# Raw block products ahead of the token sums in a seven-product down projection, and attention buffers in another order

## The chip, the cores and the metric

The kernel runs on one core of one Trainium2 chip. The metric is the device time of one execution in microseconds (us); lower is better. Before the change it is 1193.19 us, the median of three runs (1192.18 to 1194.01).

## What is computed

One layer of a hybrid encoder on 256 tokens of width 2048, everything in float32:

```python
def reference(x, ...):
    h = rms_norm(x, attn_norm[layer])
    x = x + hybrid_mixer(h, ...)        # w_in, two groups of 8 heads, w_out
    h = rms_norm(x, ffn_norm[layer])
    x = x + conv_ffn(h, ...)

def conv_ffn(h, w_up_l, conv_w_l, conv_b_l, w_down_l):
    u = h @ w_up_l                      # 2048 -> 2 * 5632
    u = causal depthwise conv, width 3 (u) + conv_b_l
    gate, val = jnp.split(u, 2, axis=-1)
    return (jax.nn.silu(gate) * val) @ w_down_l     # 5632 -> 2048
```

The mixer is a projection `w_in` (2048 to 6152 columns), softmax attention with forget gates for eight heads, stick-breaking attention for eight more, and a projection `w_out` of the normed, joined outputs.

## The kernel before

**Precision.** Each weight block arrives from memory as float32 (`w_raw`, 128 x 2048 elements, 1 MB) and is split by `split` (lines 204 to 213) into a high part `w_hi`, a cast on ScalarE (line 208), and a low part `w_lo = w_raw - w_hi`, a subtraction on VectorE (line 209). Activations are split in the same way. A product is then three matmuls: high by high, high by low, low by high. `load` (198 to 202) issues the DMA on SyncE's queue (SP). Loads and splits are traced inside `tc.high_priority(offset=AHEAD)` with `AHEAD = 200`, so that the framework's scheduler ranks them as if they stood 200 instructions earlier. The scheduler fixes the order on every engine when the kernel is built; on the chip each engine follows its list in order and waits on semaphores.

**Buffers.** `tc.tile_pool` takes a stretch of SBUF for tiles of equal tags that rotate through `bufs` buffers. A pool opened after others have closed lies over their memory, and its tiles wait until what was there is done. In the attention stage (`ExitStack` at 272) there are, in order, `wpool` (three `w_raw`, two `w_hi`, two `w_lo`), `at` (queries, keys, values, and the outputs `oT` and sums `ssq`) and `tmp` (temporaries, among them the tag "raw" that `sums_of_squares` writes with its `junk`). After it closes, `wff` (574) is opened in the same place, with four `w_raw`, three `w_hi`, three `w_lo` and one `w_sum`.

**Stages.** `w_in` and the attention heads; `w_out` in two groups (545 to 566), the second of which also makes the sums of squares and the transposed rows `hT` for the next norm; then the feed-forward part. The latter goes through 44 blocks of 128 features in six parts (`FFN_PARTS`): five of eight blocks, one of four. For each two blocks `up_pair` computes gate and value by `feature_major` (244 to 262, matmuls at 252 and 257), in two halves of 1024 input features; `convolved` does the convolution on ScalarE and VectorE; lines 765 to 769 make SiLU, the product `gate`, and its split `g2`, appended to `pairs`. From the third pair on, `combinations` (637 to 654) makes sums and differences of two pairs' token halves in `t` and splits them into `s` (lines 650 and 651); its calls make `sums[0]` (first and third pair) and `sums[1]` (second and fourth).

**The down projection runs behind.** When a part is done, its down projection is put into `behind`, and `step` (616 to 626), called after each half of `feature_major`, advances it: 14 products in the 16 halves of the next part (`pace` 14), 11 pieces in the 8 halves of the last (`pace` 22). `down_in_seven` (656 to 734) treats the part's four pairs as 2 x 2 blocks and replaces eight block products by seven of 12 matmuls each (`product`, line 675). In order, by the names used below:

- M1: weights `w11`, tokens `of_pairs(0, 0)`; M2: `w11 + w12` with `of_sums(0)`; M3: `w22` with `of_sums(2)`
- M4: `w11 + w12 + w22` with `of_sums(1)`; M5: `w12 + w22` with `of_sums(3)`
- M6: `w21` with `of_pairs(1, 0)`; M7: `w11 + w12 + w22 + w21` with `of_pairs(1, 1)`

The running sum of weights is the tile `w_sum` (one buffer), loaded with `w11` and added to on VectorE at 698, 706 and 726. `of_sums` reads `sums[0]` in the first six of its twelve matmuls and `sums[1]` in the last six; `of_pairs(1, 0)` likewise reads the third pair's `g2` and then the fourth's. `down_in_seven` runs nine times in all, each covering 1024 of the 2048 output columns; the fifth part's other 1024 columns and the last part are plain products.

Of the kernel before, what the change touches and what calls it, by code (L numbers as in the profile page):

```python
# [8 lines left out]
F32 = mybir.dt.float32  # L9
F32R = mybir.dt.float32r  # L10
AF = mybir.ActivationFunctionType
ALU = mybir.AluOpType
AX = mybir.AxisListType

P = 128
D = 2048
S = 256
# [3 lines left out]
NH = 8  # L21
# [22 lines left out]
def hybrid_layer(  # L44
# [20 lines left out]
    act, dve = nc.scalar, nc.vector  # L65
# [10 lines left out]
    psb = ctx.enter_context(tc.tile_pool(name="psb", bufs=2, space=bass.MemoryType.PSUM))  # L76

    def f32(t):
        return t.bitcast(F32)
# [37 lines left out]
    def rsqrt(out_, ss, scale, n):  # L117
        a = small.tile([P, n], F32, name="rs_a", tag=f"rs_a{n}")
        y = small.tile([P, n], F32, name="rs_y", tag=f"rs_y{n}")
        u = small.tile([P, n], F32, name="rs_u", tag=f"rs_u{n}")  # L120
        dve.tensor_scalar(a, ss, scale, EPS, op0=ALU.mult, op1=ALU.add)
        act.activation(y, a, AF.Ln)
        act.activation(y, y, AF.Exp, scale=-0.5)
        dve.tensor_tensor(u, a, y, op=ALU.mult)
        dve.tensor_tensor(u, u, y, op=ALU.mult)
        dve.tensor_scalar(u, u, -0.5, 1.5, op0=ALU.mult, op1=ALU.add)
        dve.tensor_tensor(out_, y, u, op=ALU.mult)
# [31 lines left out]
    def sums_of_squares(ss, c):  # L159

        for t in range(NT):
            junk = tmp.tile([P, 512], F32, name="junk", tag="raw", bufs=4)
            act.activation(junk, xt[t][:, c * 512 : (c + 1) * 512], AF.Square, accum_out=ss[:, t, c : c + 1])

    def token_factors(ss, n):
# [30 lines left out]


    def load(src, into=None):
        raw = into if into is not None else wpool.tile([P, 2048], F32, name="w_raw", tag="w_raw")
        a, b = src.shape[1:]  # L200
        nc.sync.dma_start(raw[:, : a * b].rearrange("p (a b) -> p a b", a=a), src)
        return raw

    def split(raw, a, b):
        hi = wpool.tile([P, 2048], F32R, name="w_hi", tag="w_hi", bufs=n_split)
        lo = wpool.tile([P, 2048], F32R, name="w_lo", tag="w_lo", bufs=n_split)
        n = a * b
        act.copy(hi[:, :n], raw[:, :n])  # L208
        dve.tensor_tensor(lo[:, :n], raw[:, :n], f32(hi[:, :n]), op=ALU.subtract)  # L209
        return (  # L210
            hi[:, :n].rearrange("p (a b) -> p a b", a=a),
            lo[:, :n].rearrange("p (a b) -> p a b", a=a),
        )
# [5 lines left out]
    def rows_of(w, k0, n, c0, cols):  # L219
        return w[k0 * P : (k0 + n) * P, c0 : c0 + cols].rearrange("(k p) c -> p k c", p=P)  # L220
# [49 lines left out]
        return t2  # L270

    with ExitStack() as actx:
        n_split = 2
        wpool = actx.enter_context(tc.tile_pool(name="wpool", bufs=3))
        at = actx.enter_context(tc.tile_pool(name="at", bufs=1))
        pss = actx.enter_context(tc.tile_pool(name="pss", bufs=2, space=bass.MemoryType.PSUM))
        tmp = actx.enter_context(tc.tile_pool(name="tmp", bufs=2))

        def project(c0, cols, **kw):
            return token_major(lambda k: hT[:, k], wi, 0, KT, c0, cols, **kw)  # L280

        def scaled(dst, ps, t):
            act.activation(dst, ps, AF.Identity, scale=rstd1[:, t : t + 1])
# [8 lines left out]
        def fox_rows(acc, dst, g):  # L292

            rows = []
            for t in range(NT):
                raw = tmp.tile([P, 512], F32, name="raw", tag="raw", bufs=4)
                scaled(raw, acc[:, t, :], t)
                rows.append(raw)
            for t in range(NT):
                raw = rows[t]  # L300
                r3 = raw.rearrange("p (h d) -> p h d", h=4)
                sq = tmp.tile([P, 512], F32, name="sq", tag="raw", bufs=4)
                dve.tensor_tensor(sq, raw, raw, op=ALU.mult)
                ss = small.tile([P, 4], F32, name="ss", tag="ss")
                dve.tensor_reduce(ss, sq.rearrange("p (h d) -> p h d", h=4), axis=AX.X, op=ALU.add)
                r = small.tile([P, 4], F32, name="r", tag="r")
                rsqrt(r, ss, 1.0 / HD, 4)
                dve.tensor_tensor(r3, r3, r.unsqueeze(2).to_broadcast([P, 4, HD]), op=ALU.mult)
            yield
            yield  # L310
            for t in range(NT):
                to_heads(dst, rows[t], t, g)
                yield

        oT = [at.tile([P, 2, S], F32R, name=f"oT{h}") for h in range(2 * NH - 4)]
        oT += [hT[:, KT - 4 + i] for i in range(4)]
        ssq = [at.tile([P, S], F32, name=f"ssq{i}") for i in range(2)]

        def attended(po, h, g, group):

# [24 lines left out]
                    transposed_split(j, ga)  # L347

        acc_q0 = project(0, 512, pieces=(2,) * 8, before=opening)
        masks = tmp.tile([P, 4 * P], F32, name="masks", tag="raw", bufs=4)  # L350
        load_parameters(masks)
        ss1 = const.tile([P, NT, 4], F32, name="ss1")
        for c in range(4):
# [216 lines left out]
    R = None  # L570


    n_split = 3
    wpool = ctx.enter_context(tc.tile_pool(name="wff", bufs=4))
    ff = ctx.enter_context(tc.tile_pool(name="ff", bufs=2))
    psf = ctx.enter_context(tc.tile_pool(name="psf", bufs=2, space=bass.MemoryType.PSUM))
    crow = ff.tile([NC2, 4, P], F32, name="crow", tag="val", bufs=1)
# [78 lines left out]
    def down_in_seven(f0, pairs, sums, c0):  # L656


        w11, w12 = (rows_of(wd, f0, 4, c0 + i * 512, 512) for i in range(2))
        w21, w22 = (rows_of(wd, f0 + 4, 4, c0 + i * 512, 512) for i in range(2))  # L660
        x11, x12 = xt[0][:, c0 : c0 + 512], xt[0][:, c0 + 512 : c0 + 1024]
        x21, x22 = xt[1][:, c0 : c0 + 512], xt[1][:, c0 + 512 : c0 + 1024]

        def of_pairs(h, t):
            return lambda a, part, j: pairs[2 * h + a][:, part, j, t * P : (t + 1) * P]

        def of_sums(q):
            return lambda a, part, j: sums[a][:, part, q, j, :]

        def product(bank, first, lhs, parts):  # L670
            hi, lo = parts
            for i in range(4):
                a, j = divmod(i, 2)
                for n, (l, r) in enumerate(((0, hi), (0, lo), (1, hi))):
                    nc.tensor.matmul(  # L675
                        bank, lhs(a, l, j), r[:, i, :], start=first and i + n == 0,
                        stop=i == 3 and n == 2, skip_group_check=not first,
                    )

        def add(to, bank, op=ALU.add):  # L680
            with tc.high_priority(offset=2 * AHEAD):
                dve.tensor_tensor(to, to, bank, op=op)

        def ahead():
            return tc.high_priority(offset=AHEAD)


        bank_a = psf.tile([P, 512], F32, name="bank_a", tag="a")
        with ahead():
            w = wpool.tile([P, 2048], F32, name="w_sum", tag="w_sum", bufs=1)  # L690
            load(w11, into=w)
            parts = split(w, 4, 512)
        product(bank_a, True, of_pairs(0, 0), parts)
        add(x11, bank_a)
        yield
        bank_b = psb.tile([P, 512], F32, name="bank_b", tag="t")
        with ahead():
            dve.tensor_tensor(w, w, load(w12), op=ALU.add)
            parts = split(w, 4, 512)
        product(bank_b, True, of_sums(0), parts)  # L700
        add(x22, bank_b)
        yield
        with ahead():
            b22 = load(w22)
            parts = split(b22, 4, 512)
            dve.tensor_tensor(w, w, b22, op=ALU.add)
        product(bank_b, False, of_sums(2), parts)
        add(x12, bank_b)
        yield
        with ahead():  # L710
            parts = split(w, 4, 512)
        product(bank_a, False, of_sums(1), parts)
        add(x12, bank_a, ALU.subtract)
        yield
        with ahead():
            b12, b22 = load(w12), load(w22)
            dve.tensor_tensor(b12, b12, b22, op=ALU.add)
            parts = split(b12, 4, 512)
        product(bank_a, False, of_sums(3), parts)
        add(x22, bank_a, ALU.subtract)  # L720
        yield
        bank_c = psb.tile([P, 512], F32, name="bank_c", tag="t")
        with ahead():
            b21 = load(w21)
            parts = split(b21, 4, 512)
            dve.tensor_tensor(w, w, b21, op=ALU.add)
        product(bank_c, True, of_pairs(1, 0), parts)
        add(x11, bank_c)
        yield
        with ahead():  # L730
            parts = split(w, 4, 512)
        product(bank_a, False, of_pairs(1, 1), parts)
        add(x21, bank_a)
        yield
# [113 lines left out]
```

## Time and profile before

The profiled execution took 1194.88 us by its own clock, with a span of 1193.1 us from the first to the last instruction. Busy times are from the same execution; the busy time of PE holds overlapping, pipelined matmuls.

| | before |
|---|---|
| median of 3 runs | 1193.19 us |
| profiled execution, its own time | 1194.88 us |
| its span | 1193.1 us |
| TensorE matmuls (PE) | 1144.6 us, 96% of the span |
| VectorE (DVE) | 904.9 us, 76% |
| ScalarE (ACT) | 616.8 us, 52% |
| DMA | 230.27 MB, mean 193 GB/s |
| mean granted TensorE clock | 0.974 |

In the profile L675 is line 675; an arrow `out<-in` gives the tiles; "[2.32 <-ACT s L650]" says that the engine sat idle 2.32 us before this instruction and that ScalarE's write of `s` at line 650 ended the wait. PE is the matmul side of TensorE, PEld its weight loads, SPq the queue in which SyncE issues DMAs. PEclk is the clock granted to TensorE as a share of full speed.

### The profile page before, as it was taken

To read this page: it belongs to the slowest core of one execution; us is meant where nothing else is said; L and a number is where in the kernel's file an instruction comes from. 1 tells how busy PE (TensorE), PEld (TensorE's weight loads), DVE (VectorE), ACT (ScalarE), POOL (GpSimd) and SP (SyncE) were. 2 spreads that over 40 slices of the span, in tenths; PEclk is the share of its full clock that TensorE was granted. 3 is DMA by queue.
4 is the path that set the end of the run, shared out by engine and by line. 5 is a ranking of instruction groups with operands and counts; after the bars stand their busy time and mean duration, and the time that the engine had idled before them with its cause. 6 is when DMAs were issued, how large, how long until landed. Compare 5 with 4: busy or idle time off the path is not lost.

```text
span 1193.1 us, 14521 instructions
## 1 busy us (share of the span) xinstructions
PE 1144.6 (96%) x5894; PEld 970.8 (81%) x5894; DVE 904.9 (76%) x978; ACT 616.8 (52%) x667; POOL 0.2 (0%) x4
## 2 busy tenths in 40 slices
PE   7999999999999899997999899998999979998998
PEld 6998888888888778886888678886888868886886
DVE  4646656565565666788899989998899989999864
ACT  4644454445654545554656445554655545554641
POOL 0000000000000000000000000000000000000000
PEclk9999999999999989998999989998999989998999
DMA  6665555555445296554768556774767657665651
GB/s 224 212 218 182 173 175 173 156 166 167 151 142 176 72 324 201 184 177 151 237 213 256 187 190 212 235 238 161 242 204 234 205 174 231 219 220 176 212 176 71
DMA packets 172046, 230.27 MB, mean 193 GB/s; under 512 B 4025, under 2 KB 117835, under 8 KB 171979
## 3 DMA queue, kind: packets, MB, share of 16 engines
q1 hardware_dynamic: 171978, 229.35, 59.3%
q8 instruction: 46, 0.75, 0.3%
q14 instruction: 22, 0.17, 0.0%
HBM read 227.23 MB, written 2.10 MB: 192 GB/s over the span
## 4 chain that ended last, share of the span: by engine, by line
PE 90%; DVE 4%; ACT 3%; DMA 2%; issue 1%; SPq 0%; ACTq 0%; DVEq 0%
PE pu L252 31%; PE pu L257 15%; PE bank_a L675 8%; PE acc L238 8%; PE acc L237 8%; PE acc L239 8%; PE bank_b L675 5%; ACT w_hi L208 2%; DVE w_lo L209 2%; PE bank_c L675 2%; PE bank_a L747 1%; PE bank_a L749 1%; PE bank_a L748 1%; PE ps_x L148 1%; DMA x<-in_x_dram 0%
## 5 line engine op out<-in xcount | busy, mean ns | idle before, releaser
L209 DVE TENSOR_TENSOR w_lo<-w_raw,w_hi 128x2048 fp32r<-128x2048 f32 (+2 forms) x195 | 429.7, 2203 | 184.0 <-ACT w_hi L208 183.5
L208 ACT CAST w_hi<-w_raw 128x2048 fp32r<-128x2048 f32 (+2 forms) x195 | 358.6, 1840 | 339.0 <-PE pu L252 116.8
L252 PE MATMUL pu<-hT,w_hi 128*128 128x512 f32 x1664 | 527.5, 398 | 0.4 <-ACT w_hi L208 0.4
L257 PEld LDWEIGHTS pu<-hT,w_lo 128*128 128x128 f32 x1664 | 314.8, 189 | 76.0 <-DVE w_lo L209 1.8
L257 PE MATMUL pu<-hT,w_lo 128*128 128x256 f32 x1664 | 330.2, 280 | 1.1 <-DVE w_lo L209 1.1
L252 PEld LDWEIGHTS pu<-hT,w_hi 128*128 128x128 f32 x1664 | 261.0, 190 | 6.9 <-ACT w_hi L208 0.7
L237 PE MATMUL acc<-w_hi,hT 128*128 128x512 f32 (+1 forms) x320 | 120.4, 376 | 0.0
L238 PE MATMUL acc<-w_lo,hT 128*128 128x512 f32 (+1 forms) x320 | 119.2, 373 | 0.6 <-DVE w_lo L209 0.6
L239 PE MATMUL acc<-w_hi,hT 128*128 128x512 f32 (+1 forms) x320 | 119.0, 372 | 0.0
L208 ACT CAST w_hi<-w_sum 128x2048 fp32r<-128x2048 f32 x36 | 68.7, 1909 | 68.7 <-PE pu L252 46.5
L209 DVE TENSOR_TENSOR w_lo<-w_sum,w_hi 128x2048 fp32r<-128x2048 f32 x36 | 82.3, 2287 | 14.0 <-ACT w_hi L208 14.0
L675 PE MATMUL bank_b<-w_hi,s 128*128 128x512 f32 x144 | 58.7, 466 | 17.2 <-ACT s L650 10.3
L238 PEld LDWEIGHTS acc<-w_lo,hT 128*128 128x128 f32 x320 | 60.6, 189 | 9.7 <-DVE w_lo L209 1.5
L239 PEld LDWEIGHTS acc<-w_hi,hT 128*128 128x128 f32 x320 | 60.6, 189 | 8.8
L237 PEld LDWEIGHTS acc<-w_hi,hT 128*128 128x128 f32 x320 | 60.8, 190 | 8.1
L675 PE MATMUL bank_a<-w_hi,s 128*128 128x512 f32 x144 | 51.6, 418 | 9.8 <-ACT w_hi L208 9.8
L675 PEld LDWEIGHTS bank_b<-w_hi,s 128*128 128x128 f32 x144 | 31.9, 226 | 27.9 <-ACT s L650 11.8
L675 PE MATMUL bank_a<-w_hi,g 128*128 128x512 f32 x144 | 48.1, 395 | 0.0
L675 PEld LDWEIGHTS bank_a<-w_hi,s 128*128 128x128 f32 x144 | 28.4, 197 | 18.7 <-ACT w_hi L208 12.8
L606 DVE SCALAR_TENSOR_TENSOR gate<-up,ccol,gate 128x256 f32<-128x256 f32 x88 | 38.6, 481 | 3.6 <-ACT gate L601 3.4
L606 DVE SCALAR_TENSOR_TENSOR val<-up,ccol,val 128x256 f32<-128x256 f32 x88 | 38.2, 480 | 0.9 <-ACT val L601 0.7
L237 PE MATMUL acc<-w_hi,oT 128*128 128x512 f32 x96 | 38.1, 397 | 0.0
(186 smaller groups left out, 1182.3 us busy)
## 6 DMA issues: line engine op xcount, KB each, us to landing
w_raw<-in_w_up_dram SPq DMA_DIRECT2D x88, 1024.0 KB, 5.2
w_raw<-in_w_down_dram SPq DMA_DIRECT2D x53, 1024.0 KB, 5.1
w_raw<-in_w_in_dram SPq DMA_DIRECT2D x36, 1024.0 KB, 5.1
w_raw<-in_w_out_dram SPq DMA_DIRECT2D x16, 1024.0 KB, 5.1
w_sum<-in_w_down_dram SPq DMA_DIRECT2D x9, 1024.0 KB, 5.2
w_raw<-in_w_in_dram SPq DMA_DIRECT2D x12, 688.0 KB, 4.0
w_raw<-in_w_in_dram SPq DMA_DIRECT2D x8, 512.0 KB, 3.9
out_dram<-x SPq DMA_DIRECT2D x8, 256.0 KB, 2.5
```

What stands on the lines that cost most here:

```text
L148: nc.tensor.transpose(ps[:, j, t * P : (t + 1) * P], xt[t][:, (k + j) * P : (k + j + 1) * P], ident)
L208: act.copy(hi[:, :n], raw[:, :n])
L209: dve.tensor_tensor(lo[:, :n], raw[:, :n], f32(hi[:, :n]), op=ALU.subtract)
L237: nc.tensor.matmul(o, lhi, hi[:, i, :], start=first, stop=False)
L238: nc.tensor.matmul(o, lhi, lo[:, i, :], start=False, stop=False)
L239: nc.tensor.matmul(o, llo, hi[:, i, :], start=False, stop=last)
L252: nc.tensor.matmul(acc[:, j, :], hi[:, i, j * P : (j + 1) * P], hT[:, k].rearrange("p a b -> p (a b)"), start=k == 0, stop=False,)
L257: nc.tensor.matmul(acc[:, j, S:], lo[:, i, j * P : (j + 1) * P], hT[:, k, 0, :], start=False, stop=k == KT - 1,)
L606: dve.scalar_tensor_tensor(a[:, j, :], u[:, j, w : w + S], ccol[:, w, f : f + 1], a[:, j, :], op0=ALU.mult, op1=ALU.add,)
L675: nc.tensor.matmul(bank, lhs(a, l, j), r[:, i, :], start=first and i + n == 0, stop=i == 3 and n == 2, skip_group_check=not first,)
L747: nc.tensor.matmul(acc[t], g[:, 0, ts], hi[:, i, :], start=first, stop=False)
L748: nc.tensor.matmul(acc[t], g[:, 0, ts], lo[:, i, :], start=False, stop=False)
```

## The change

Two things are changed.

**The order in `down_in_seven`.** M6 moves to second place, straight after M1: its own load and split of `w21`, its product into `bank_c`, its addition to `x11`. M2, M3, M4 and M5 follow as they were. M7 loads `w21` a second time and adds it to the running sum itself. The order becomes M1, M6, M2, M3, M4, M5, M7. Count and kind of matmuls, splits and additions stay; each of the nine calls issues one more 1 MB load.

**Pools.** In the attention stage `wpool` is divided into `wraw`, `whi` and `wlo`, opened after `at` and `tmp`; a last pool, `late`, takes the tag "raw" (with `junk` and `masks`), the outputs `oT` and the sums `ssq`. In the feed-forward stage `wff` becomes `wlo2`, `whi2`, `wraw2` and `wsum`, opened in this order. The numbers of buffers are the same as before.

```diff
     def sums_of_squares(ss, c):
...
-            junk = tmp.tile([P, 512], F32, name="junk", tag="raw", bufs=4)
+            junk = late.tile([P, 512], F32, name="junk", tag="raw", bufs=4)
...
-        wpool = actx.enter_context(tc.tile_pool(name="wpool", bufs=3))
         at = actx.enter_context(tc.tile_pool(name="at", bufs=1))
         pss = actx.enter_context(tc.tile_pool(name="pss", bufs=2, space=bass.MemoryType.PSUM))
         tmp = actx.enter_context(tc.tile_pool(name="tmp", bufs=2))
+        wraw = actx.enter_context(tc.tile_pool(name="wraw", bufs=3))
+        whi = actx.enter_context(tc.tile_pool(name="whi", bufs=2))
+        wlo = actx.enter_context(tc.tile_pool(name="wlo", bufs=2))
+        late = actx.enter_context(tc.tile_pool(name="late", bufs=1))
...
-        oT = [at.tile([P, 2, S], F32R, name=f"oT{h}") for h in range(2 * NH - 4)]
+        oT = [late.tile([P, 2, S], F32R, name=f"oT{h}") for h in range(2 * NH - 4)]
...
-    wpool = ctx.enter_context(tc.tile_pool(name="wff", bufs=4))
+    wlo = ctx.enter_context(tc.tile_pool(name="wlo2", bufs=3))
+    whi = ctx.enter_context(tc.tile_pool(name="whi2", bufs=3))
+    wraw = ctx.enter_context(tc.tile_pool(name="wraw2", bufs=4))
+    wsum = ctx.enter_context(tc.tile_pool(name="wsum", bufs=1))
...
         product(bank_a, True, of_pairs(0, 0), parts)
         add(x11, bank_a)
         yield
+        bank_c = psb.tile([P, 512], F32, name="bank_c", tag="t")
+        with ahead():
+            parts = split(load(w21), 4, 512)
+        product(bank_c, True, of_pairs(1, 0), parts)
+        add(x11, bank_c)
+        yield
         bank_b = psb.tile([P, 512], F32, name="bank_b", tag="t")
...
-        bank_c = psb.tile([P, 512], F32, name="bank_c", tag="t")
         with ahead():
-            b21 = load(w21)
-            parts = split(b21, 4, 512)
-            dve.tensor_tensor(w, w, b21, op=ALU.add)
-        product(bank_c, True, of_pairs(1, 0), parts)
-        add(x11, bank_c)
-        yield
-        with ahead():
+            dve.tensor_tensor(w, w, load(w21), op=ALU.add)
             parts = split(w, 4, 512)
         product(bank_a, False, of_pairs(1, 1), parts)
         add(x21, bank_a)
```

More of the change, by code (lines that the diff above doesn't have):

```diff
@@ L198, in load @@
     def load(src, into=None):
-        raw = into if into is not None else wpool.tile([P, 2048], F32, name="w_raw", tag="w_raw")
+        raw = into if into is not None else wraw.tile([P, 2048], F32, name="w_raw", tag="w_raw")
         a, b = src.shape[1:]
@@ L204, in split @@
     def split(raw, a, b):
-        hi = wpool.tile([P, 2048], F32R, name="w_hi", tag="w_hi", bufs=n_split)
-        lo = wpool.tile([P, 2048], F32R, name="w_lo", tag="w_lo", bufs=n_split)
+        hi = whi.tile([P, 2048], F32R, name="w_hi", tag="w_hi")
+        lo = wlo.tile([P, 2048], F32R, name="w_lo", tag="w_lo")
         n = a * b
@@ L272, in hybrid_layer @@
     with ExitStack() as actx:
-        n_split = 2
-        wpool = actx.enter_context(tc.tile_pool(name="wpool", bufs=3))
         at = actx.enter_context(tc.tile_pool(name="at", bufs=1))
@@ L295, in fox_rows @@
             for t in range(NT):
-                raw = tmp.tile([P, 512], F32, name="raw", tag="raw", bufs=4)
+                raw = late.tile([P, 512], F32, name="raw", tag="raw", bufs=4)
                 scaled(raw, acc[:, t, :], t)
@@ L301, in fox_rows @@
                 r3 = raw.rearrange("p (h d) -> p h d", h=4)
-                sq = tmp.tile([P, 512], F32, name="sq", tag="raw", bufs=4)
+                sq = late.tile([P, 512], F32, name="sq", tag="raw", bufs=4)
                 dve.tensor_tensor(sq, raw, raw, op=ALU.mult)
@@ L313, in fox_rows @@
                 yield
-        oT = [at.tile([P, 2, S], F32R, name=f"oT{h}") for h in range(2 * NH - 4)]
+        oT = [late.tile([P, 2, S], F32R, name=f"oT{h}") for h in range(2 * NH - 4)]
         oT += [hT[:, KT - 4 + i] for i in range(4)]
-        ssq = [at.tile([P, S], F32, name=f"ssq{i}") for i in range(2)]
+        ssq = [late.tile([P, S], F32, name=f"ssq{i}") for i in range(2)]
         def attended(po, h, g, group):
@@ L349, in hybrid_layer @@
         acc_q0 = project(0, 512, pieces=(2,) * 8, before=opening)
-        masks = tmp.tile([P, 4 * P], F32, name="masks", tag="raw", bufs=4)
+        masks = late.tile([P, 4 * P], F32, name="masks", tag="raw", bufs=4)
         load_parameters(masks)
@@ L570, in hybrid_layer @@
     R = None
-    n_split = 3
-    wpool = ctx.enter_context(tc.tile_pool(name="wff", bufs=4))
+    wlo = ctx.enter_context(tc.tile_pool(name="wlo2", bufs=3))
+    whi = ctx.enter_context(tc.tile_pool(name="whi2", bufs=3))
+    wraw = ctx.enter_context(tc.tile_pool(name="wraw2", bufs=4))
+    wsum = ctx.enter_context(tc.tile_pool(name="wsum", bufs=1))
     ff = ctx.enter_context(tc.tile_pool(name="ff", bufs=2))
@@ L689, in down_in_seven @@
         with ahead():
-            w = wpool.tile([P, 2048], F32, name="w_sum", tag="w_sum", bufs=1)
+            w = wsum.tile([P, 2048], F32, name="w_sum", tag="w_sum")
             load(w11, into=w)
```

## The prediction

> **What bounds the kernel.** I read the page first, then the time table by stage, the waits of PE, the timeline around them, and the chain at the border of the stages. The page's busy shares and the chain say TensorE:
>
> ```profile
> PE 1144.6 (96%) x5894; PEld 970.8 (81%) x5894; DVE 904.9 (76%) x978; ACT 616.8 (52%) x667; POOL 0.2 (0%) x4
> ...
> PE 90%; DVE 4%; ACT 3%; DMA 2%; issue 1%; SPq 0%; ACTq 0%; DVEq 0%
> ```
>
> The table by stage (stretch, its length, busy us of PE, PEld, DVE, ACT, POOL, granted clock, DMA share, GB/s) shows where it is not:
>
> ```profile
> 412.00:423.00 11.00, 5.41 (x21) 3.41 (x21) 7.01 (x18) 6.85 (x12) 0.00 (x0) 0.74 0.85 272
> 423.00:525.00 102.00, 102.00 (x577) 88.82 (x576) 74.27 (x80) 50.98 (x51) 0.00 (x0) 0.98 0.66 215
> ...
> 663.40:802.40 139.00, 133.01 (x682) 112.03 (x681) 126.04 (x121) 76.11 (x67) 0.00 (x0) 0.96 0.65 212
> ...
> 556.00:671.00 115.00, 115.00 (x614) 98.08 (x613) 107.06 (x100) 66.99 (x58) 0.00 (x0) 1.00 0.68 220
> 533.40:556.00 22.60, 16.63 (x69) 12.89 (x68) 18.76 (x22) 9.06 (x9) 0.00 (x0) 0.77 0.56 186
> ```
>
> One hole at the entry of the feed-forward stage (412 to 428 us) and one at the start of each later part. Between holes TensorE is full at clock 1.00, and VectorE stands at 93% (107.06 of 115).
>
> **The size of the holes.** In the chain, products with an up half between them start 8.38 us apart (607.58, 615.96, 624.34), with two halves 13.96 us apart (585.24, 599.20). A product of twelve matmuls takes 2.80 us, so an up half 5.58. A part of 14 products and 16 halves is 39.2 + 89.3 = 128.5 us. M1 starts at 525.34, 663.43, 802.37 and 940.21. From M1 to M4 (its row of eleven, one matmul back) it should be 3 x 8.38 = 25.1 us and was 34.8, 35.6, 34.5 and 35.5: lost 9.6, 10.5, 9.4 and 10.3, mean 9.95. In the last part, from M1 (1073.27) to M5 (1111.61), 38.3 us stand for 27.9: lost 10.4. At the entry, 413.13 to 427.89, the work at full pace (ten up matmuls of each kind 3.5 us, eight transposes 0.9, four matmuls for `R` 0.6) is 5.0 of 14.8: lost 9.8. Together 60 us, the most that the change can win.
>
> **Why the parts start badly.** PE's waits (total, times, longest), then ScalarE, VectorE and PE in order of time at the first hole:
>
> ```profile
> PE bank_b L675 <- ACT s L650: 10.3, 5, 2.3
> PE bank_a L675 <- ACT w_hi L208: 9.8, 5, 2.0
> PE bank_b L675 <- DVE s L651: 6.9, 5, 1.7
> ```
>
> ```profile
> 538.64 0.69 DVE L766 TENSOR_TENSOR gate<-gate,val 128x512 f32<-128x512 f32 x1
> ...
> 540.04 0.69 DVE L769 TENSOR_TENSOR g<-gate,g 128x512 fp32r<-128x512 f32 x1
> ...
> 542.48 2.29 DVE L209 TENSOR_TENSOR w_lo<-w_raw,w_hi 128x2048 fp32r<-128x2048 f32 x1 [0.96 <-ACT w_hi L208]
> 543.02 0.50 PE L675 MATMUL bank_b<-w_hi,s 128*128 128x512 f32 x1 [2.32 <-ACT s L650]
> 544.69 1.29 DVE L651 TENSOR_TENSOR s<-t,s 128x512 fp32r<-128x512 f32 x2
> 545.43 1.22 PE L675 MATMUL bank_b<-w_hi,s 128*128 128x512 f32 x2 [1.66 <-DVE s L651]
> 549.49 0.79 PE L675 MATMUL bank_a<-w_hi,s 128*128 128x512 f32 x1 [1.99 <-ACT w_hi L208]
> ```
>
> M2 starts at 533.7, does its six matmuls on `sums[0]`, and its other six, put behind an up half (until 540.5), wait for the low part of `s`, ready at 545.4. Then M4's cast waits for the buffers that M2 kept. Idle 2.32 + 1.66 + 1.99 = 5.97 us; the loss is 9.6 because matmuls run at half pace until about 551 (granted clock 0.56 in 545 to 555). So a us of idle costs 9.6 / 5.97 = 1.61 us here. [...]
>
> **The change at the part starts.** M6 takes M2's place. It needs no `s`, but the fourth pair's `g2` (L768, L769), ready at 540.7. Of VectorE's weight work ahead of that, M2's addition and subtraction (L698 and L209, 2 x 2.29) give way to one subtraction: `g2` comes 2.29 us earlier, 538.4, and `s` at 543.1. M6's second six are due at 535.1, or at 540.5 if put behind the up half as M2's were: idle between 3.3 us and none. M2 then comes 8.38 us later, its second six at 533.7 + 2.8 + 5.6 + 1.4 = 543.5, just behind `s`. From this side the loss is 0 to 3.3 x 1.61 = 5.3 us.
>
> From VectorE's side: its busy time per part, 126.2 us, is all kept. A part can't be shorter than 128.5 by TensorE, and there VectorE would be 98% busy, though its own waits for casts take 7.9 us in the 115 full ones. If half of these remain a part takes 130.2, if all, 134.1. I take 132.7, nearer the upper end because casts are released by TensorE and the queue is in order: 4.2 us lost in place of 9.95, a gain of 5.75 x 4 = 23.0. In the last part VectorE is busy almost without a gap from 1050 to 1101, so only the one addition that leaves the front counts: 2.3 of 10.4 (bounds 0 and 10.4).
>
> **The second load of `w21`.** Nine loads of 5.1 us (page, 1 MB down loads), 9.4 MB. DMA share is 0.65 in a part; two more loads on 28 make it 0.70 to 0.72. M7 now has load, addition, cast and subtraction in a row: 5.1 + 2.3 + 1.9 + 2.3 = 11.6 us. Its cover is M5's step and the up half: a down load goes out far ahead (SP's timeline: `b21` at 619.39 for M6 at 641.09, 21.7 us), and the cast waits for TensorE's buffer anyway (640.95 after the up half, 3.44 us). Behind it in SP's queue stands the next `w11` load, which waits for M7's subtraction (643.08 to 645.3, load at 645.39, product at 663.43); cast and subtraction after landing need until 654.7, so 8 us of room. I price it at 0. Without cover, the load and the addition show: 7.4 us x 9 = 67; a gain is excluded, since it adds work alone.
>
> **The pools.** The chain and SP's waits at the entry:
>
> ```profile
> 412.89 0.24 PE acc L239
> 413.13 0.02 issue
> 413.15 4.99 DMA w_raw<-in_w_up_dram
> 418.14 0.02 issue
> 418.16 1.91 ACT w_hi L208
> 420.07 0.02 issue
> 420.09 2.30 DVE w_lo L209
> ```
>
> ```profile
> SPq L201 <- DVE w_lo L209: 21.9, 2, 17.8
> SPq L201 <- PE acc L239: 7.5, 1, 7.5
> ```
>
> The first up load waited for the last `w_raw` to be split (405.65), then 7.5 us more for the last `w_out` matmul: `wff` lies over `w_hi`, `w_lo` and `oT`, which that matmul reads. By the tile sizes (at 36 KB and tmp 21 KB a partition, three `w_raw` 24 KB) `wraw2`, at 48 to 80 KB, lies over tmp and `wraw` alone, and `wlo2`, `whi2` over at and tmp, done with the heads. So the load goes at 405.65, its high part is there at 412.6 and its low part at 414.9 in place of 422.4. I take 7.5 of the 9.8. Bounds: 9.8, and -1.9 (still waiting, and one cast ahead of the last rows of `hT` on ScalarE). TensorE is full until 525, so what is won stays won.
>
> **Sum.** 7.5 + 23.0 + 2.3 + 0 = 32.8; span 1193.1 - 32.8 = 1160.3. The profiled execution's own time is 1.8 us over its span, and 1.7 over the median; off the median of 1193.2 the forecast is **1160 us**, its own range 1150 to 1172.
>
> **Rivals.**
> - *Full gain.* VectorE's waits vanish as it falls behind, and M6's second half is put behind the up half: 9 at the entry, 9 x 4, 6 in the last part: 1142. For it: casts are mostly done before VectorE comes. Against: 98% on an in-order queue. 0.10.
> [...]
> - *The wait moves from M2 to M6.* `g2` comes no earlier than now, M6 isn't put behind the up half: idle 535.1 to 540.7, 5.6 x 1.61 = 9.0 lost per start. Only the entry and 1 us per start remain: 1193 - 7.5 - 5 = 1181. 0.20.
> - *The pools do nothing* (the load still waits for TensorE): 1168. 0.07.
> - *M7 is late.* Of its 7.4 us, 3.5 show per call, about the room a split has before its use elsewhere: 9 x 3.5 = 31, which undoes the rest: 1192. 0.07.
> - *Slower: `g2` behind the sums' weight work.* M2's addition and subtraction (4.6 us) are ranked 200 instructions ahead and now may stand in front of L766 to L769 on VectorE: `g2` at 545.3, M6 idle 10.2 us, lost 16.4 per start, 6.5 more than now, x 5 - 7.5 = +25: 1218. It decides once `g2` is over 1.5 us later than now (540.7): then 7.1 idle, 11.4 lost, times five, eats the entry. For it: L209 stands in front of `s` today. [...] 0.16.
>
> The forecast has 0.30. A measurement of this kernel tells 0.2% (2.4 us) from none. Faster: 0.30 + 0.10 + 0.10 + 0.20 + 0.07 and 0.01 of M7's = 0.78; same 0.06; slower 0.16. The range 1140 to 1192 leaves out the slower case and the best of the full gain.
>
> **What would show it.** Right: the first up load issued near 405.7; no PE wait on `s` at L675; parts of 130 to 134 us with VectorE above 94%; the extra load followed by no wait of M7. Wrong: a wait of M6 for L768 or L769 over 5 us; clock under 0.9 around the starts; M7's matmuls waiting for L209 or a DMA.

## The result and the profile after

The changed kernel takes 1155.57 us (median of four runs, 1154.68 to 1160.24) beside 1193.6 us before (four runs, 1192.18 to 1194.02). The ratio is 0.9691, 95% interval 0.9664 to 0.9719. The profiled execution is the slowest of the four: 1160.24 us by its own clock, span 1158.5 us, 34.6 us under the span before. Line numbers below are of the changed kernel: the product is at L680, its addition to `x` at L687, the split of `s` at L655 and L656, that of `g` at L772 and L773, the additions of weights at L709 (for M2), L717, L728 (for M5) and L734 (for M7).

The page of the kernel after, busy times and the chain by engine:

```profile
PE 1130.7 (98%) x5894; PEld 960.7 (83%) x5894; DVE 902.9 (78%) x978; ACT 614.2 (53%) x667; POOL 0.2 (0%) x4
...
PE 91%; DVE 4%; ACT 2%; DMA 2%; issue 1%; SPq 0%; ACTq 0%; DVEq 0%
```

VectorE's work is the same (902.9 for 904.9 us), but in 34.6 us less. At the entry of the feed-forward stage, the chain of the kernel after (start, us, what):

```profile
403.80 1.92 ACT w_hi L208
405.73 0.02 issue
405.75 2.30 DVE w_lo L209
408.05 0.02 issue
408.07 5.08 DMA w_raw<-in_w_up_dram
...
413.23 1.92 ACT w_hi L208
415.15 0.02 issue
415.17 2.30 DVE w_lo L209
417.47 0.04 issue
417.52 0.50 PE pu L257 x2
```

The first up load no longer waits for TensorE's last `w_out` matmul (7.5 us before): it goes out 0.02 us after VectorE has split the last `w_raw`. PE's waits of the kernel after (total, times, longest):

```profile
PE bank_a L680 <- ACT w_hi L208: 8.8, 4, 3.7
PE bank_c L680 <- ACT g L772: 4.3, 1, 4.3
```

Every wait on `s` is gone. Two others stand in their place. Stretches of the kernel after (stretch, length, busy us of PE, PEld, DVE, ACT, POOL, granted clock, DMA share, GB/s):

```profile
560.00:634.00 74.00, 74.00 (x394) 63.01 (x393) 72.32 (x67) 41.40 (x36) 0.00 (x0) 1.00 0.81 269
...
652.00:784.00 132.00, 130.01 (x680) 110.33 (x679) 125.54 (x121) 75.15 (x67) 0.00 (x0) 0.99 0.72 239
...
620.00:636.00 16.00, 16.00 (x86) 13.65 (x85) 15.45 (x19) 9.56 (x8) 0.00 (x0) 1.00 0.93 307
636.00:639.00 3.00, 1.01 (x5) 0.49 (x4) 3.00 (x3) 2.72 (x3) 0.00 (x0) 1.00 0.91 314
639.00:643.00 4.00, 4.00 (x14) 3.38 (x15) 4.00 (x5) 0.19 (x1) 0.00 (x0) 0.57 0.78 262
643.00:650.00 7.00, 7.00 (x42) 6.11 (x41) 5.19 (x5) 3.80 (x5) 0.00 (x0) 1.00 0.44 145
```

Inside a part VectorE is busy 72.32 of 74 us, TensorE all of it. M1 starts (its row of eleven, one matmul back) at 519.3, 651.7, 784.0, 918.3 and 1041.2: parts of 132.4, 132.3 and 134.3 us for 137.8 to 138.9. From the fourth start to the fifth it is 122.9 us for 133.2; one up half of 5.58 us fewer stands between, so the floor there is 122.9. The longest holds a slow transfer: in the chain, the load for M7 takes 8.22 us at 876.71, for 5.1 elsewhere.

The first of the new holes, in the timeline of the kernel after:

```profile
636.50 0.40 PE L680 MATMUL bank_a<-w_hi,g 128*128 128x512 f32 x1
636.93 1.90 ACT L208 CAST w_hi<-w_sum 128x2048 fp32r<-128x2048 f32 x1
...
638.88 0.50 PE L680 MATMUL bank_a<-w_hi,g 128*128 128x512 f32 x1 [1.99 <-ACT w_hi L208]
```

At 636.50 the last matmul of M7 begins, and it ends 0.40 us later. The matmul at 638.88 is the first of the next part's M1: the scheduler has put it, alone of its twelve, ahead of two up halves (it is hoisted), and it waits for the cast at 636.93, which starts right after M7 has let its weight buffer go. This happens at three borders, with waits of 1.99, 1.99 and 3.74 us. At the third, ScalarE's copies ahead of the cast waited for VectorE's split of `s` (L656), and the cast began at 903.46, 1.8 us after M7's end; whether the slow transfer 27 us earlier made VectorE late isn't shown. After the first wait, the table above shows a mean clock of 0.57 over 4 us. With the floor of 128.5 us, a wait of 1.99 and 3.41 us at half clock (1.7 us lost) make 132.2 us, the length of the first two parts. The fourth wait of that line, 1.06 us, is in the last part.

### The profile page after: what moved, and what is told of

The parts are those of the page before. It is cut to its first block, busy times and chain, and to the rows that moved or that the text cites. A ratio compares the mean times of both kernels' runs of the same rounds, so it can differ in the third digit from the quotient of the medians.

```text
span 1158.5 us, 14545 instructions
## 1 busy us (share of the span) xinstructions
PE 1130.7 (98%) x5894; PEld 960.7 (83%) x5894; DVE 902.9 (78%) x978; ACT 614.2 (53%) x667; POOL 0.2 (0%) x4
## 4 chain that ended last, share of the span: by engine, by line
PE 91%; DVE 4%; ACT 2%; DMA 2%; issue 1%; SPq 0%; ACTq 0%; DVEq 0%
PE pu L252 31%; PE pu L257 16%; PE bank_a L680 8%; PE acc L238 8%; PE acc L237 8%; PE acc L239 8%; PE bank_b L680 4%; DVE w_lo L209 2%; PE bank_c L680 2%; ACT w_hi L208 2%; DMA w_raw<-in_w_down_dram 1%; PE bank_a L751 1%; PE bank_a L752 1%; PE bank_a L753 1%; PE ps_x L148 1%
## 5 line engine op out<-in xcount | busy, mean ns | idle before, releaser
L237 PE MATMUL acc<-w_hi,hT 128*128 128x512 f32 (+1 forms) x320 | 121.2, 379 | 0.0
L238 PEld LDWEIGHTS acc<-w_lo,hT 128*128 128x128 f32 x320 | 60.7, 190 | 10.6 <-DVE w_lo L209 1.2
L237 PEld LDWEIGHTS acc<-w_hi,hT 128*128 128x128 f32 x320 | 60.7, 190 | 9.3
L680 PE MATMUL bank_a<-w_hi,g 128*128 128x512 f32 x144 | 48.6, 398 | 7.7 <-ACT w_hi L208 7.7
L680 PE MATMUL bank_a<-w_hi,s 128*128 128x512 f32 x144 | 48.3, 396 | 1.1 <-ACT w_hi L208 1.1
L680 PE MATMUL bank_b<-w_hi,s 128*128 128x512 f32 x144 | 48.7, 397 | 0.0
L680 PEld LDWEIGHTS bank_a<-w_hi,g 128*128 128x128 f32 x144 | 27.0, 187 | 14.7 <-ACT w_hi L208 9.0
L268 ACT COPY t<-pu 128x512 f32<-128x512 f32 x52 | 30.0, 580 | 15.7 <-PE pu L257 11.2
L237 PE MATMUL acc<-w_hi,oT 128*128 128x512 f32 x96 | 38.0, 396 | 0.0
```

Of the source, the lines that this page charges most:

```text
L237: nc.tensor.matmul(o, lhi, hi[:, i, :], start=first, stop=False)
L238: nc.tensor.matmul(o, lhi, lo[:, i, :], start=False, stop=False)
L268: act.copy(t2, acc[:, :, S:])
L680: nc.tensor.matmul(bank, lhs(a, l, j), r[:, i, :], start=first and i + n == 0, stop=i == 3 and n == 2, skip_group_check=not first,)
```

## Experiments

All times are medians beside runs of the kernel before on the same chip (1192.7 to 1193.6 us). "Old" names the kernel before.

**Which part brings how much.** `e1_order` is the old kernel with the new order alone; `e2_pools` has the new pools alone.

> The new order of the seven products alone (M6 second, second load of w21 in M7), pools as before. If the two parts of the change add up, the entry of the feed-forward stage loses its 9.8 us again and the rest stays: about 1163 us, and M2 no longer waits for s at the start of any part. Rival: without the earlier loads the new order gains less, since everything at the part starts hangs together: above 1170 us.

> The new pools alone, the old order. Theory: the first up load goes out when the last raw block of w_out is split, some 7.5 us earlier, and nothing else changes: about 1187 us, with the five waits of M2 for s as before (2.3 and 1.7 us each). Rival: the heads' stage has lost 2 us to the new placement (w_out's loads begin at 345.65 in the changed kernel, at 343.63 before), so the net is only 5 to 6 us: 1188 us. If the pools do nothing: 1193 us.

Measured: the order 1161.5 us (0.9733, 0.9719 to 0.9748), the pools 1188.39 us (0.9955, 0.9941 to 0.997). That is 32.1 and 5.2 us; together 37.3, and both at once brought 38.0: the parts add up. In the profile of `e1_order` M1 starts at 524.2, 656.6, 787.3, 919.6 and 1042.4: over the four starts 29.9 us are gained (518.2 for 548.1), in the last part 2.0. PE's waits of `e1_order` are those of the full change without its pools:

```profile
PE bank_a L675 <- ACT w_hi L208: 7.2, 4, 2.0
PE bank_c L675 <- ACT g L767: 4.3, 1, 4.3
```

With the pools alone, the first M1 starts at 519.2 for 525.2 and the waits on `s` remain (10.6 and 6.4 us). The first up load goes out 5.3 us earlier (407.88 for 413.15), not 7.5: in the attention stage the ninth of the sixteen `w_out` loads already goes out 1.8 us later (345.47 for 343.63), so that stage itself lost about 2 us. The prediction had no term for this loss (see `e7_pad`).

**The second load of `w21`.** Old order and old pools; only M7 reloads `w21` and adds it itself.

```diff
-            b21 = load(w21)
-            parts = split(b21, 4, 512)
-            dve.tensor_tensor(w, w, b21, op=ALU.add)
+            parts = split(load(w21), 4, 512)
...
+            dve.tensor_tensor(w, w, load(w21), op=ALU.add)
             parts = split(w, 4, 512)
```

> The old order and old pools, but M7 loads w21 a second time and adds it itself, as in the change; nothing else. It prices the nine extra loads. Theory: hidden, 1193 us within 2. Rival (M7 is late): 3.5 us for each of nine calls, up to 1225 us, with M7's matmuls waiting for L209 or a DMA.

1189.43 us (0.9966, 0.9953 to 0.9979): the load isn't merely hidden, the version is 4.2 us faster. The last part's M1 stands where it stood (1072.8 for 1073.3), and its M7 starts at 1123.7 for 1128.4: the gain lies in the last part's start. There, in the kernel before (and by its line numbers), the addition of 2.29 us (L726, at 1096.21) stood in VectorE's queue ahead of the second half of `s` (L647 and L651); with it gone, one wait for `s` less is left (four for five), and the clock stands at half for 3.4 us in place of 10.2.

**The hoisted matmul.** The changed kernel, with M1's terms in the order low, high, low by high.

```diff
-        product(bank_a, True, of_pairs(0, 0), parts)
+        product(bank_a, True, of_pairs(0, 0), parts, "lhh")
```

> The changed kernel, but M1 takes its low-part weights first (lo, hi, lo-by-hi in place of hi, lo, lo-by-hi for each block), so that its first matmul can't be placed two up halves early; same work, same sum. Theory: the 2.0 to 3.7 us waits of that one matmul for its cast, with the half clock behind them, are all that is left at three of the part borders: 3 x 3.9 = 12 us less, 1144 us, parts of 128.5 us. Rival: VectorE sets the parts of 132 us (98% busy at 128.5), and the loss turns up elsewhere: 1153 to 1156 us.

1154.27 us (0.9673, 0.9657 to 0.9689; 1153.85 to 1154.95), no difference from the change that these intervals tell. No matmul is hoisted now, and the wait on the cast falls to 1.1 us in all. PE's waits of `e4_lo_first`:

```profile
PE pu L252 <- DVE t L269: 6.1, 3, 2.0
```

At the same three borders TensorE now waits for VectorE to empty an up half's PSUM. Parts take 130.8, 132.3 and 130.8 us. Take one wait away and the next stands there, 2.03 us for 1.99: the rival held.

These parts also show the price of such a wait. The first wait, and two stretches behind the first and the second of them, in `e4_lo_first`:

```profile
637.74 0.71 PE L252 MATMUL pu<-hT,w_hi 128*128 128x512 f32 x2 [2.03 <-DVE t L269]
...
638.00:642.00 4.00, 4.00 (x25) 3.47 (x25) 4.00 (x5) 0.38 (x1) 0.00 (x0) 1.00 0.78 262
769.00:773.00 4.00, 4.00 (x16) 3.51 (x15) 3.92 (x4) 0.65 (x2) 0.00 (x0) 0.59 0.72 260
```

The waits are equal, but the clock stayed after the first (the part is 2.3 us over the floor of 128.5) and fell after the second (3.8 us over it). In `e1_order` it fell at the first and third border and stayed at the second: parts of 132.4, 130.7 and 132.3 us. Within one profile the clock's falls lie whole multiples of 3.413 us apart (in the kernel after at 639.37, 772.49 and 905.61, each 39 such steps from the next; in the kernel before at 417.31, 543.60 and 683.55, with 37 and 41 steps between). Thirteen single waits of 1.99 to 2.03 us stand at part borders in the kernel after, `e1_order`, `e4_lo_first`, `e7_pad` and `e8_plain_first`. The eight that lie within one step were followed by 3.41 us at half clock; the five that a boundary between steps cuts in two, the longer piece at most 1.80 us, were not. So the same wait costs about 2.2 or 3.9 us, by where it happens to lie.

**Is it VectorE's amount of work?** As `e4_lo_first`, without the multiplication by `R`: the sum is written straight into `up`. This kernel leaves that factor of the layer out.

```diff
-        t2 = summed(ff, ps, "t2")
-        dve.tensor_tensor(u[:, :, 2:], t2, R.unsqueeze(1).to_broadcast([P, 2, S]), op=ALU.mult)
...
+            act.copy(t2, ps[:, :, S:])
+            dve.tensor_tensor(u[:, :, 2:], ps[:, :, :S], t2, op=ALU.add)
```

> The version with M1's terms in the order low, high, low by high (1154.3 us), and the multiplication of the up products by R left out: ScalarE and VectorE only add the two halves of PSUM, VectorE does one operation less per up pair. Theory, VectorE sets the length of the parts (126.4 busy of 130.8 us): its busy time falls by about 4 to 5 us a part, the parts fall to 128.5 to 129.5 us, the wait of the up matmuls for VectorE's emptying (L269, 6.1 us in all) is gone, time about 1145 to 1149. Rival, it is the order of the matmuls and the casts of ScalarE that set the parts: periods stay at 130.8 to 132.3, time 1153 to 1155.

1139.81 us (0.9553, 0.9537 to 0.9569), below what either theory gave. A stretch of `e5_no_r` and the same of `e4_lo_first`, in this order:

```profile
650.00:780.00 130.00, 130.00 (x691) 110.73 (x690) 122.89 (x114) 77.13 (x67) 0.00 (x0) 1.00 0.75 247
```

```profile
650.00:780.00 130.00, 127.97 (x670) 108.65 (x669) 123.45 (x115) 73.93 (x65) 0.00 (x0) 0.99 0.72 241
```

M1 starts at 518.0, 646.5, 775.0 and 903.4: every part takes 128.5 us, the 14 products and 16 halves at full pace that the prediction had worked out as the floor. So 0.68 us less per up pair on VectorE (5.5 us a part) clears all waits of the starts, and 6.0 us more in the last part (106.1 for 112.1 us). What is left of the holes hangs on VectorE. The multiplication is also one step in the chain from an up product to the convolution; whether the smaller amount of work did it or the shorter chain isn't separated here.

**M6 first.** The changed kernel with the blocks of M1 and M6 exchanged.

> The changed kernel with M6, not M1, as the first product of a part. Theory, what a part's first product must not need is anything that the end of the part before has just begun to make: M6 needs g of the fourth pair of tokens, which is ready some 7 us after the first product would start, so a wait for g returns at the product's line (2 to 4 us at each of the borders), the parts take 136 to 139 us, and the time is 1172 to 1185. Rival, only the sums of tokens are late and any product with raw tokens does as well: parts of 132 to 134 us and 1154 to 1158.

1171.35 us (0.9816, 0.9801 to 0.9832), parts of 136.6 to 136.8 us. The size is the theory's, the wait isn't. PE's waits of `e6_m6_first`:

```profile
PE bank_c L680 <- DVE w_lo L209: 10.6, 4, 3.1
PE bank_c L680 <- ACT w_hi L208: 7.1, 3, 2.4
```

It waits for the split of the weights, and hardly for `g` (0.7 us in all). Here four of M6's matmuls are hoisted ahead of the two up halves, the first of them in need of the cast, the second of the subtraction: 2.37 and 3.08 us of waiting at the first border, where one hoisted matmul cost 1.99 us. So the reason given for M6 isn't what happened: its other eight matmuls stand behind the two halves (656.04 at the first border) and find `g` ready. The price goes with how many matmuls the scheduler pulls up; these two cases are all that was seen of it.

**Where the attention stage lost 2 us.** As `e4_lo_first`, with 832 unused bytes ahead of the attention's `wraw`.

```diff
+        pad = actx.enter_context(tc.tile_pool(name="pad", bufs=1))
+        pad.tile([P, 208], F32, name="pad")
         wraw = actx.enter_context(tc.tile_pool(name="wraw", bufs=3))
```

> The version with M1's terms reordered (1154.3 us), with 832 bytes of unused memory before the w_raw buffers, so that they and the weight buffers behind them start at other addresses. Theory, the 233 ns from one matmul of the w_in and w_out stages to the next (226 to 227 before the change) come from where the weight buffers lie: with other addresses the step is 227 ns again, and the time 1152. Rival, they come from something else in the new pools (which buffers are shared, how many there are): 233 ns and 1154.

The chain of `w_in` matmuls in three kernels (start, us, what): before, after, and `e7_pad`.

```profile
99.96 0.23 PE acc L237
...
101.09 0.23 PE acc L239
```

```profile
99.85 0.23 PE acc L238
...
101.02 0.23 PE acc L237
```

```profile
99.91 0.23 PE acc L237
...
101.04 0.23 PE acc L239
```

Five steps each: 1.13 us before, 1.17 after, 1.13 with the pad, that is 226, 234 and 226 ns. So the addresses decide the step, as the theory says, and the ninth `w_out` load goes out at 342.90, for 344.47 in `e4_lo_first`, 345.65 after and 343.63 before. (`e4_lo_first` and the kernel after have the same attention stage, so executions differ by about 1 us there.) The time didn't follow: 1154.47 us (0.9674, 0.9659 to 0.9688). M1 starts at 517.1 for 518.2 in `e4_lo_first`, and this 1.1 us is lost again at the third border, where a wait of 2.78 us with half clock behind it stands for 2.03 us without (133.1 us for 130.8). What it is in the address that matters isn't settled.

**Plain products first in the last part.** As `e4_lo_first`, the fifth part's plain products (four pieces, three in the expectation) ahead of its seven. The plain products also take their terms low part first, which the expectation doesn't name.

```diff
-                        nc.tensor.matmul(acc[t], g[:, 0, ts], hi[:, i, :], start=first, stop=False)
-                        nc.tensor.matmul(acc[t], g[:, 0, ts], lo[:, i, :], start=False, stop=False)
+                        nc.tensor.matmul(acc[t], g[:, 0, ts], lo[:, i, :], start=first, stop=False)
+                        nc.tensor.matmul(acc[t], g[:, 0, ts], hi[:, i, :], start=False, stop=False)
...
-            behind.append(down_in_seven(f_lo, pairs, sums, 0))
...
                 behind.append(down_plain(f_lo, pairs, 1024, 1024))
+                behind.append(down_in_seven(f_lo, pairs, sums, 0))
```

> The version with M1's terms reordered (1154.3 us), and in the last part the three plain products of the remaining columns put before its seven block products. Theory, the last part loses 8.3 us at its start because M5 and M6 need sums and g of the last tokens that are only being made; with the plain products in front these are ready, the hole falls to 2 to 4 us: 1148 to 1151. Rival, the plain products need the same g and the wait only moves to them: 1153 to 1156.

1157.23 us (0.9695, 0.9681 to 0.971): a little above the rival's range. From M7 of the part before to the end it takes 122.2 us for 120.5. The rival's reason didn't come: the plain products that were moved wait 1.3 us, for the weights' low part. The wait for `g` now stands in the last part's own projection (L237), at 1131.45:

```profile
PE acc L237 <- ACT g L772: 3.1, 1, 3.1
```

**Taking work off VectorE with an engine that is idle.** Three versions of `e7_pad`, in each of which one kind of VectorE instruction goes to GpSimd: the addition ahead of M5 (`b12 + b22`, called M6's in the expectation), the four small ones ahead of `s`, and the multiplication by `R`.

```diff
-            dve.tensor_tensor(b12, b12, b22, op=ALU.add)
+            nc.gpsimd.tensor_tensor(b12, b12, b22, op=ALU.add)
```

> The padded version (1154.5 us) with the addition of two weight blocks ahead of M6 (b12 and b22, 2.29 us, two a part) moved from VectorE to GpSimd, which is idle. Theory, VectorE's load is all that matters: 4.6 us less a part, about what leaving out R took (5.3 us, 14.5 us won): 1141 to 1147. Rival, the two engines hinder each other: VectorE's other instructions of 2.29 us become longer or start later while GpSimd adds, and the time stays or rises, 1154 to 1165. [...]

> The padded version (1154.5 us) with the four small additions and subtractions ahead of the token sums (0.42 us each, eight a part, 3.3 us) moved from VectorE to GpSimd. Theory, VectorE's load is all that matters: 3.3 us less a part, two thirds of what leaving out R took: 1144 to 1148. Rival, the chain through four of them becomes so slow that the sums are late at M2 (product line waits for s again) or VectorE is held up meanwhile: 1154 to 1162.

> The padded version (1154.5 us) with the multiplication of the up products by R (0.68 us, eight a part, 5.5 us) moved from VectorE to GpSimd. Theory, VectorE's load is all that matters: as without that multiplication, 1139 to 1143. Rival, GpSimd takes longer than VectorE for it and the two hinder each other; the convolution behind it comes late, and the time is 1154 to 1175.

All three are slower than `e7_pad`: 1162.73 us (0.9745, 0.9727 to 0.9763), 1161.57 (0.9738, 0.9722 to 0.9753) and 1161.22 (0.9733, 0.971 to 0.9756). The timeline of `e9_gpsimd_w` shows why that one is:

```profile
680.20 2.28 DVE L209 TENSOR_TENSOR w_lo<-w_raw,w_hi 128x2048 fp32r<-128x2048 f32 x1
680.21 6.73 POOL L730 TENSOR_TENSOR w_raw<-w_raw 128x2048 f32<-128x2048 f32 x1 [64.78 <-DVE x L689]
682.40 5.22 DVE L613 SCALAR_TENSOR_TENSOR gate<-up,ccol,gate 128x256 f32<-128x256 f32 x2
687.54 0.47 DVE L613 SCALAR_TENSOR_TENSOR val<-up,ccol,val 128x256 f32<-128x256 f32 x1
```

Two convolution steps that take 0.48 us each elsewhere last 5.22 us together; the first took 4.82 of them, until just behind GpSimd's end (686.94). GpSimd in turn took 6.73 us where its shortest took 4.59, which fits its having first let VectorE's subtraction of 2.28 us end. In this stretch the two took turns, a whole instruction at a time, with 4.82 us for the longest of these steps. In `e11_gpsimd_r` GpSimd takes 2.13 us for what VectorE does in 0.68, and VectorE's subtractions of 2.29 us last up to 3.38. In `e10_gpsimd_s` VectorE's subtractions hardly lengthen (2.29 us on average, 2.75 at most), but the four small ones take 5.5 us on GpSimd for 1.7; that this is the cause there isn't shown. As the moved work came back as waiting or as a longer chain, these runs don't tell VectorE's amount of work from the chain either.

**Freeing PSUM by ScalarE.** As `e7_pad`; ScalarE copies both halves, VectorE adds from the copy. The temporaries `t` of `combinations` take the same buffer (not shown).

```diff
-        t2 = summed(ff, ps, "t2")
+        t4 = ff.tile([P, 2, 2 * S], F32, name="t4", tag="t4", bufs=1)
+        t2 = t4[:, :, :S]
+        with tc.high_priority(offset=2 * AHEAD):
+            act.copy(t4, ps)
+            dve.tensor_tensor(t2, t2, t4[:, :, S:], op=ALU.add)
```

> The padded version (1154.5 us) in which ScalarE copies both halves of an up pair's PSUM (one copy of 1024 columns in place of one of 512, one buffer of 4 KB in place of two of 2 KB), and VectorE adds the halves from the copy. VectorE's work is the same; only what frees PSUM moves from VectorE (L269) to ScalarE. Theory, it is the coupling that costs: TensorE no longer waits for VectorE's emptying, the parts come near 128.5 to 130 us and the time is 1146 to 1151. Rival, it is VectorE's amount of work (126 of 131 us a part): the wait moves to g, to s or to the weight buffers that VectorE frees, and the time is 1153 to 1158. A third way: the single buffer holds ScalarE's queue up until VectorE has multiplied, the casts behind it come late, and the time is above 1160.

1161.11 us (five runs; 0.9733, 0.972 to 0.9746): the third way. PE's waits of `e12_act_copy`:

```profile
PE pu L252 <- ACT t L606: 13.6, 4, 4.2
```

The copy itself is late now, because its one buffer is free only when VectorE has multiplied (ScalarE waits 15.3 us for that). Whether two such buffers would remove the coupling wasn't tried.

No version is shown to beat the change: `e4_lo_first` and `e7_pad` have the lowest medians of those that compute everything, 1.3 and 1.1 us below it, inside the spread of its runs.

## Why the prediction was right, and where not

The forecast was 1160, the time 1155.57: within its own range of 1150 to 1172, and the mechanism is the one forecast. By its steps:

**Entry, 7.5 us.** The mechanism is right: the load went 0.02 us behind the last split, as worked out from the tile sizes, though at 408.07 and not near 405.7. The size was too high. Net 6.0 us came (M1 at 519.2 with the pools alone, for 525.2), because the new addresses cost the attention stage about 2 us, a term that the sum didn't have. The prediction had counted the pools only by who waits for whom.

**Four part starts, 5.75 us each.** The mechanism is right, the term mis-sized. The prediction left 4.2 us lost at each start. In `e1_order`, where no slow transfer disturbs it, the parts exceed their floor (128.5, and 122.9 for the fourth) by 3.9, 2.2, 3.8 and 0.0: 2.5 us each, 29.9 us gained for 23.0. In the profiled run of the change it is 26.2. The bound "from VectorE's side" was the one to take: VectorE is 125.54 of 132 us busy (95%), and with 5.5 us less on it (`e5_no_r`) the rest is gone. What didn't come is the place. The prediction let TensorE wait for VectorE somewhere; it waits for the cast of M1's hoisted matmul, and once that is gone, for L269. Nor is the price in proportion to the idle time, as the 1.61 us for each us of idle had it: a wait of about 2 us cost 2.2 or 3.9 us, by whether the clock fell. (Before, at the first hole, the half clock lasted until 553.8, not 551.) One sign that the prediction had named for being wrong did come: a clock under 0.9 around the starts (0.57 over 639 to 643). That the fourth start loses nothing at all wasn't foreseen.

**Last part, 2.3 us.** To the last matmul it is 2.0 in `e1_order` and 2.1 in the profiled run; M6 waits there 4.3 us for `g`, the only place where it does. `e3_reload` shows that more can be had by moving the one addition alone, 4.2 us, with M6 left where it was.

**Second load, 0.** Right: in the profile after no matmul of M7 waits, DMA share 0.72 as worked out. That a gain is excluded was wrong: with the old order the edit brought one (`e3_reload`), as it also moves an addition.

**The sum.** 32.8 us was forecast for the span; the profiled run has 34.6 (5.9 + 26.2 + 2.1, and 0.4 behind the last matmul), the medians 38.0, which is 6.0 + 29.9 + 2.0 from the single parts, 37.9. The profiled run is 3.7 us short of `e1_order` in the part starts: 2.0 us at the third border, where it waited 1.75 us longer, and 1.6 at the second, where the clock fell as it didn't in `e1_order`. The other three executions have no profile; that their starts went as in `e1_order` isn't shown.

**The rivals.** *Full gain* (1142) needs VectorE's waits to vanish; only with less work on VectorE did the parts reach 128.5. The second 0.10 among the chances stands for remaining waits that leave the clock alone; no run shows that a wait does so by being short. A single wait of 1.99 us at the first border of the kernel after was followed by 3.4 us at half clock; of the thirteen waits of 1.99 to 2.03 us eight were, and five kept the clock. *The wait moves to M6* is true of the last part alone (4.3 us). *The pools do nothing* and *M7 is late* are refuted by `e2_pools` and `e3_reload`. The slower case, `g2` behind the sums' weight work, didn't occur: M6 never waits for `g` at the start of a full part, even as the first product in `e6_m6_first` (0.69 us, in the last part), which remains 22 us faster than the kernel before.

## What to carry to other kernels

When the products that need fresh results are moved behind those that don't, work out next which engine's total remains per part: here VectorE, at 95% of a 132 us part, held the last 2 to 4 us, and taking away one wait of TensorE only showed the next. Look at what the scheduler pulls ahead of a border, matmul by matmul; one hoisted matmul cost 2 us of waiting and, where the clock fell, 3.4 us of half clock. Before a change of 2 us is put down to an edit, see whether the clock fell in both profiles. Moving VectorE's work to the idle GpSimd made the kernel 6.8 to 8.3 us slower than `e7_pad` here: before an idle engine is counted as free capacity for a full one, see in a trace whether both run at once.

## What the runs showed of the hardware

- The step of a 512-column matmul in `w_in` was 226 ns before, 234 after, and 226 again with 832 unused bytes ahead of the weight buffers.
- In `e9_gpsimd_w` GpSimd and VectorE held each other up for whole instructions: a step of VectorE of 0.48 us lasted up to 4.82 us, and GpSimd's addition 6.73 us, where its shortest took 4.59.
- Of thirteen single waits of TensorE of 1.99 to 2.03 us, eight were followed by 3.41 us at half clock and five by none; the eight lay within one of the 3.41 us steps on which the clock changed, the five across a boundary of them.
